# One hybrid gMLP and SSM layer on one core: gate and bias sums moved to VectorE, w_out's last weights and x fetched in another order, and a quarter of the last LayerNorm on two other engines

## Chip, cores and metric

The kernel runs on one core of a Trainium2 chip. The metric is the device time of one execution in microseconds, as the median of several runs.

## What is computed

One trunk layer of a diffusion backbone, all in fp32 on 1024 tokens of width 2048, with a context of 256 tokens in front. What matters here is the modulation by `c`, the bias of the spatial gating, and the end:

```python
mod_x = silu(c) @ w_ada + b_ada                      # c: (1, 2048), w_ada: (2048, 6144)
shift_x, scale_x, gate_x = split(mod_x, 3)
proj_x = modulate(layer_norm(x), shift_x, scale_x) @ w_in          # (1024, 5120)
...
# group A: gMLP, per head h of 8 and chunk of 128 positions
v = layer_norm(gelu(v)) * ln_g + ln_b
mixed = einsum("hpq,bnqhd->bnphd", w_s, v) + b_s
ya = gelu(u) * mixed * silu(za)
# group B: bidirectional S5 SSM over context and latents, D skip, GELU, GLU
yb = s5(ub, ub_ctx) * silu(zb)
out = concat([ya, yb]) @ w_out                       # (1024, 2048) @ (2048, 2048)
return layer_norm(ALPHA * x + gate_x * out) * ln_g + ln_b
```

The kernel takes `ln_b` of the gating through the spatial matrix ahead of time: what it adds to `mixed` for a head is `b_s` plus the row sums of `w_s` times `ln_b`. Those row sums are the "bias sums" here. The "gate row" is the third part of `mod_x`, 2048 numbers, needed only at the end.

## The kernel before

Every large matmul runs in three passes on split operands: a weight chunk of 128 x 1024 (512 KB) is loaded by SP's DMA queue into one of two raw buffers `wraw` (L565), ScalarE (ACT) copies it to a rounded `whi`, and VectorE (DVE) subtracts to get the rest, `wlo`. There are two buffers of each. `Weights` (L554) does this in the order of one list, `chunks`: `load_to(i)` issues loads up to chunk i, `split_to(i)` the splits. A load needs the raw buffer that the split two chunks earlier gave back. Per chunk TensorE (PE) then does 24 matmuls of 128x512.

The order of the program is: a prologue (modulation by `c`, LayerNorm of x), blocks of the input projection (`v`, `zb`, the context block `cx`, `ub`, then `v`, `u`, `za` and `zb` in turn), the spatial gating, the GLU, and the out stage. Side work is written as Python generators in a list `tasks`; `pump` takes the next step of these after every few main matmuls, so each engine's instruction order is fixed when the program is built. A generator says how far it wants to be behind: `until(t)` yields until a modelled clock of PE (`ck.pe`) or VectorE (`ck.dve`) has come to t, `wait(n)` yields n times. All compute instructions go through one metering helper, so that their line in the profile is L519.

`bias_task` (L1045) runs in the context stage: it loads the transposed spatial matrix `ws`, sums it over partitions with two fp32 matmuls against a matrix of ones (tile `io` in the rows, into a `sy` bank), and adds the result to `b_sp` by eight VectorE instructions. `gate_task` (L1062) runs in the last `zb` blocks: GpSimd's queue loads `w_gate` in 32 pieces `gw` of 128x1024 (input rows on partitions), VectorE accumulates them, each times one column of scalars `sc`, into `acc`, and four fp32 ones-matmuls into `ps` sum over the partitions. The row goes to a scratch in DRAM, from which the out stage loads it.

The out stage is two halves h of four token tiles of 128, and in each half four blocks n = 0, 2, 4, 6 of 512 output columns (`out_block`, L1426, 8 chunks each, 192 matmuls). The first half's results are taken through the residual and LayerNorm by `ln_task` during the second half, with ScalarE for the normalizing and, for the last step of it, GpSimd's addition of `lnb` over 128x1024, and written out by L1503 in pieces of 1 MB. At chunk 0 of each block `flush` issues the residuals that are left of the block before, and `gate(n)` then loads the gate columns `gt` (L1417) on SP's queue; there is one `gt` buffer, so the load waits for the last residual of the block before, and what stands behind it on the queue waits too. `z1_task` loads x for the second half: eight pieces of 128x1024 on SP's queue, one per two steps of `pump`, in block n=0 of the second half.

The last block (h=1, n=6) is done token tile by token tile. For that its eight chunks of `w_out` have to be split and kept ahead of time, in one tile `w6`. Their loads are interleaved with those of block n=4 one to one, so n=4 loads and splits 16 chunks. For each tile t = 4 to 7 comes the residual of its last quarter, the LayerNorm factors (`ln_finish`), and `finish`: for each stretch of columns one VectorE instruction `z<-z,lnw,lng` and one `z<-z,lnw,lnb` (scalar-tensor-tensor with a column of scalars `lnw`), then the output DMA. The last tile takes 1024, 512 and 512 columns.

Of the kernel before, what the change touches and what calls it, by code (L numbers as in the profile page):

```python
# [24 lines left out]
def dap(t, offset, ap):  # L25
    return bass.AP(tensor=t.tensor, offset=t.offset + offset, ap=[list(a) for a in ap])
# [559 lines left out]
def build(tc, a, out, scratch):  # L586
    nc = Metered(tc.nc)
    ck = nc.clock
    V, S, T, P, SP = nc.vector, nc.scalar, nc.tensor, nc.gpsimd, nc.sync
# [13 lines left out]
    def bank(tag, bufs):  # L603
        return (sb[1] if tag == "sb" else pp).tile([128, 512], FT, name=tag, tag=tag, bufs=bufs)
# [16 lines left out]
    def add(key, src):  # L621
        first[key] = len(chunks)
        chunks.append(src)
# [8 lines left out]
    for h in range(2):  # L632
        for n in range(0, 8, 2):
            if (h, n) != (1, 6):
                for c in range(8):
                    add(("out", h, n, c), a["w_out"][n // 2, c])
                    if (h, n) == (1, 4):
                        add(("out", 1, 6, c), a["w_out"][3, c])
    W = Weights(nc, wpool, chunks)
    last, w6 = [first["out", 1, 6, c] for c in range(8)], []  # L640

# [26 lines left out]
    tasks = []  # L668
# [366 lines left out]
    o = block(("v", 3))  # L1035
# [6 lines left out]
    cl_es.close()  # L1042
    us_es = ExitStack()
    us_p = us_es.enter_context(tc.tile_pool(name="us", bufs=2))
    def bias_task():  # L1045

        ws = st_p.tile([128, 8, 128], FT, name="ws", tag="sta")
        P.dma_start(ws, dap(a["w_sp"], 0, [[128, 128], [16384, 8], [1, 128]]))
        bs = st_p.tile([128, 8, 128], FT, name="bs", tag="stb")
        P.dma_start(bs, dap(a["b_sp"], 0, [[0, 128], [128, 8], [1, 128]]))  # L1050
        yield from until(ck.pe + 20000)
        for h0 in (0, 4):
            rs = bank("sy", 1)
            T.matmul(rs, ones, ws[:, h0:h0 + 4].rearrange("p h d -> p (h d)"), start=True, stop=True)
            yield from wait(2)
            for h in range(h0, h0 + 4):
                V.scalar_tensor_tensor(bs[:, h], rs[:, 128 * (h - h0):128 * (h - h0) + 128], vecs[:, 1, h:h + 1],
                                       bs[:, h], op0=OP.mult, op1=OP.add)
            yield from until(ck.pe + 4000)
        S.dma_start(dap(scratch["bp"], 0, [[128, 128], [16384, 8], [1, 128]]), bs)  # L1060

    def gate_task(p):  # L1062

        for c in range(2):
            cols = slice(1024 * c, 1024 * c + 1024)
            acc = p.tile([128, 1024], FT, name="acc")
            w = {}

            def load(i):
                w[i] = p.tile([128, 1024], FT, name="gw", bufs=4)  # L1070
                P.dma_start(w[i], a["w_gate"][i * 128:i * 128 + 128, cols])
            for i in range(3):
                load(i)
            yield from until(ck.pe + 3500)
            for i in range(16):
                if i < 13:
                    load(i + 3)
                if i:
                    V.scalar_tensor_tensor(acc, w[i], sc[:, 0, i:i + 1], acc, op0=OP.mult, op1=OP.add)
                else:  # L1080
                    V.tensor_scalar(acc, w[0], sc[:, 0, 0:1], None, op0=OP.mult)
                yield from wait(1 + i % 2)
            br = p.tile([128, 1024], FT, name="gw", bufs=4)
            SP.dma_start(br[0:1], a["b_gate"][None, cols])
            yield from until(ck.dve + 4000)
            for h in halves:
                ps = bank("ps", 1)
                T.matmul(ps, ones, acc[:, h], start=True, stop=True)
                yield from until(ck.pe + 1000)
                V.tensor_add(br[0:1, h], ps[0:1], br[0:1, h])  # L1090
            SP.dma_start(scratch["gate"][None, cols], br[0:1])


    tasks.append(bias_task())
    for m in range(8):
        e = bank("sb", 2)
        for c in range(2):
# [14 lines left out]
    us_es.close()  # L1112
    cx_es.close()
    ub_m = []


    def ub_there(u):
# [308 lines left out]
    def out_block(h, n, z):  # L1426

        o = [bank(*x) for x in ((("mm", 4),) * 4 if n % 4 else
                                (("sb", 2), ("sb", 2), ("ps", 1), ("sy", 1)))]
        for c in range(8):  # L1430
            if (h, n) == (1, 4):
                i = first["out", h, n, c]
                hl = W.get(i)
                W.load_to(i + 1)
                if c == 4:
                    drain(lt)
                    w6.append(z0_p.tile([128, 8, 1024], FR, name="w6", tag="z0", bufs=1))
                W.split_to(i + 1)
                W.load_to(i + 3)
                W.split_to(min(i + 2, last[7]))  # L1440
            else:
                hl = wget(("out", h, n, c))
            if c == 0:
                flush()
                gt = gate(n)
            w = [[x[:, 512 * kk:512 * kk + 512] for x in hl] for kk in range(2)]
            for i in range(4):
                for j in range(2):
                    kk, t = (i // 2, 2 * (i % 2) + j) if c < 7 else (j, i)
# [64 lines left out]
    for t in range(4, 8):  # L1514
        o = bank("mm", 4)
        for c in range(8):
            for kk in range(2):
                out_mm(o, (8 + 2 * c + kk) % 16, [x[:, kk * 512:kk * 512 + 512] for x in wts[c]], t,
                       c == 0 and kk == 0, c == 7 and kk == 1)
        residual(6, t, z1[t - 4, 1][:, 512:1024], o, gt)  # L1520
        ln_finish(t, t + 1)
        for i, x, y in ((0, 0, 1024), (1, 0, 1024)) if t < 7 else ((0, 0, 1024), (1, 0, 512), (1, 512, 1024)):
            z, c = z1[t - 4, i][:, x:y], slice(1024 * i + x, 1024 * i + y)
            for _ in finish(t, z, c, False):
                pass
            SP.dma_start(out[t * 128:t * 128 + 128, c], z)
# [6 lines left out]
def host(i):  # L1533

    C = np.ascontiguousarray
    o = s5_host(i)
    o["x"], o["ctx"] = C(i["x"][0]), C(i["ctx"][0])
    o["cc"] = C(np.stack([i["c"][0].reshape(16, 128).T, i["c_ctx"].reshape(16, 128).T], axis=1))
    w = i["w_ada"][0]

    w2 = w[:, :4096].reshape(4, 4, 128, 2, 8, 256)
    o["w_mod"] = C(w2.transpose(4, 0, 2, 1, 3, 5).reshape(8, 4, 128, 4, 512))
    o["w_gate"] = C(w[:, 4096:])
    b = i["b_ada"][0]
    o["b_mod"] = C(b[:4096].reshape(2, 8, 2, 128).transpose(3, 1, 0, 2).reshape(128, 8, 4))
    o["b_gate"] = C(b[4096:])
# [6 lines left out]
    o["w_sp"] = C(i["w_spatial"][0].transpose(0, 2, 1))  # L1553
    o["b_sp"] = C(i["b_spatial"][0])
    o["ln_g"], o["ln_b"] = C(i["ln_g"][0]), C(i["ln_b"][0])
    return o


SCRATCH = dict(gate=(2048,), bp=(8, 128, 128), pf=(8, G, 2, 128), tab=(2, 128, G, F), z5=(G, 16, 2, 144), ub=(G, 16, 8, KL), ubc=(G, 16, 8, KC), y5=(1024, 1024),
               v=(8, 128, 8, 128), ya=(8, 128, 1024), sz=(8, 128, 1024))  # L1560


# [21 lines left out]
```

## Time and profile before

| | us |
|---|---|
| median of 3 runs | 1612.44 (1611.13 to 1613.03) |
| the profiled execution | 1615.11 |
| its span, first to last instruction | 1613.3 |
| PE busy | 1567.1 |
| DVE, ACT, POOL busy | 1077.7, 504.3, 185.5 |
| out stage, second half, blocks n = 0, 2, 4, 6 | 44.83, 44.72, 49.51, 43.51 |
| from the last matmul to the end | 12.8 |

PE is the engine with work nearly all the time; matmuls of 512 columns follow each other every 0.2266 us at the full granted clock. Rows of one timeline that carry a count (x2) stand for neighbours of the same form put together; the time of such a row runs to the modelled end of the last of them, which overlaps the start of the next row. A bracket at a row's end is the idle time before it and what ended it.

### The profile page before, as it was taken

The numbers are of one execution on the slowest core, as the hardware profiler recorded it, in microseconds if no ns is written. First come the engines' busy times: TensorE is split into PE (matmuls) and PEld (weight loads), VectorE is DVE, ScalarE is ACT, GpSimd is POOL, SyncE is SP. The second block draws the span as 40 slices with busy tenths as digits, with TensorE's granted clock in tenths as the row PEclk, the third lists the DMA queues.
The fourth block names the chain that finished last, engine by engine and source line by source line (L and its number), as shares of the span: only waits on it lengthen the run. The fifth ranks groups of instructions, "written<-read, shape, count | busy, mean of one in ns | idle before, by whom it ended". The sixth has DMA issues, their size and how long they took to land.

```text
span 1613.3 us, 22086 instructions
## 1 busy us (share of the span) xinstructions
PE 1567.1 (97%) x8340; PEld 1260.7 (78%) x8340; DVE 1077.7 (67%) x1968; ACT 504.3 (31%) x832; POOL 185.5 (11%) x288
## 2 busy tenths in 40 slices
PE   4999999999999999999999999999999999999996
PEld 2556878887888888888888888888888888877775
DVE  8542646973988889888898898156565633466557
ACT  2554652112222333233233323211633412133210
POOL 0000000000222222222222222111000000012000
PEclk9999999999999999999999999999999999999998
DMA  9895454424454444444434443377544543364422
GB/s 336 323 325 173 161 173 144 148 109 127 109 125 128 114 128 129 100 127 128 127 98 128 129 117 90 138 248 248 190 143 170 196 137 124 107 230 179 137 86 104
DMA packets 133316, 251.36 MB, mean 156 GB/s; under 512 B 53973, under 2 KB 73557, under 8 KB 131417
## 3 DMA queue, kind: packets, MB, share of 16 engines
q1 hardware_dynamic: 111016, 207.68, 39.6%
q0 software_dynamic: 16672, 32.83, 7.2%
q10 hardware_dynamic: 5520, 9.44, 1.7%
q8 instruction: 65, 1.06, 0.3%
q14 instruction: 43, 0.34, 0.1%
HBM read 213.60 MB, written 36.12 MB: 155 GB/s over the span
## 4 chain that ended last, share of the span: by engine, by line
PE 84%; DMA 6%; DVE 5%; ACT 2%; SPq 1%; issue 1%; ACTq 0%; DVEq 0%
PE mm L519 64%; PE sb L519 9%; PE sy L519 8%; PE ps L519 3%; DMA wraw<-in_w_out_dram 2%; DVE wlo L519 2%; DMA ada<-in_w_mod_dram 1%; ACT whi L519 1%; DVE z L519 1%; DVE stats L519 1%; DVE xn L519 1%; DMA xn<-in_x_dram 1%; DMA wraw<-in_w_in_dram 1%; DMA ubb<-in_b_c_dram 0%; DMA cl<-in_ctx_dram 0%
## 5 line engine op out<-in xcount | busy, mean ns | idle before, releaser
L519 PE MATMUL mm<-xT,whi 128*128 128x512 f32 x2496 | 687.2, 395 | 2.0 <-ACT whi L519 1.0
L519 PEld LDWEIGHTS mm<-xT,whi 128*128 128x128 f32 x2496 | 461.6, 188 | 108.8 <-issue 7.8
L519 PE MATMUL mm<-xT,wlo 128*128 128x512 f32 x1248 | 391.0, 390 | 0.1
L519 DVE TENSOR_TENSOR wlo<-wraw,whi 128x1024 fp32r<-128x1024 f32 (+1 forms) x164 | 201.1, 1228 | 275.8 <-ACT whi L519 275.0
L519 ACT ACTIVATE whi<-wraw 128x1024 fp32r<-128x1024 f32 (+1 forms) x164 | 170.1, 1039 | 403.9 <-PE mm L519 215.4
L519 PEld LDWEIGHTS mm<-xT,wlo 128*128 128x128 f32 x1248 | 234.3, 188 | 50.9 <-DVE wlo L519 1.4
L519 DVE TENSOR_TENSOR p<-sb,ue 128x640 f32<-128x640 f32 x64 | 49.8, 819 | 49.0 <-PE sb L519 48.9
L519 PE MATMUL mm<-whi,yb 128*128 128x512 f32 x256 | 80.0, 389 | 0.0
L519 PE MATMUL mm<-y,whi 128*128 128x512 f32 x256 | 68.4, 389 | 0.0
L519 POOL TENSOR_TENSOR zs<-zs,dsk 128x16 f32<-128x16 f32 x32 | 17.7, 552 | 424.3 <-ACT zs L519 424.3
L519 PE MATMUL mm<-whi,ya 128*128 128x512 f32 x192 | 59.6, 389 | 0.0
L519 PE MATMUL sy<-ada,cs 128*32 128x512 f32 x256 | 40.5, 645 | 19.3 <-DMA ada<-in_w_mod_dram 19.2
L519 POOL TENSOR_TENSOR z<-z,lnb 128x1024 f32<-128x1024 f32 x8 | 19.2, 2397 | 347.1 <-DMA z<-in_x_dram 312.3
L519 PEld LDWEIGHTS mm<-y,whi 128*128 128x128 f32 x256 | 48.0, 188 | 10.0
L519 PEld LDWEIGHTS mm<-whi,yb 128*128 128x128 f32 x256 | 48.1, 188 | 10.0
L519 DVE TENSOR_TENSOR xT<-xm,xT 128x512 fp32r<-128x512 f32 x32 | 22.1, 692 | 45.9 <-ACT xT L519 44.3
L519 PE MATMUL mm<-wlo,yb 128*128 128x512 f32 x128 | 49.9, 390 | 0.4 <-DVE wlo L519 0.4
L519 DVE TENSOR_TENSOR_SCAN p<-ur,p 128x640 f32<-128x640 f32 x32 | 47.7, 1490 | 3.0 <-DVE ut L519 0.5
L519 PE MATMUL sb<-whi,yb 128*128 128x512 f32 x128 | 45.4, 396 | 1.4 <-ACT whi L519 1.4
L519 PE MATMUL sb<-cT,whi 128*128 128x512 f32 x128 | 46.2, 401 | 0.1
L403 POOL DMA_DIRECT2D tmp_z<-zs x64 | 44.1, 691 | 11.4 <-POOL zs L519 9.1
L519 DVE TENSOR_TENSOR p<-p,ue 128x512 f32<-128x512 f32 x64 | 44.2, 690 | 1.7
(274 smaller groups left out, 2313.2 us busy)
## 6 DMA issues: line engine op xcount, KB each, us to landing
wraw<-in_w_in_dram SPq DMA_DIRECT2D x89, 512.0 KB
ada<-in_w_mod_dram SPq DMA_DIRECT2D x64, 512.0 KB
wraw<-in_w_out_dram SPq DMA_DIRECT2D x64, 512.0 KB
gw<-in_w_gate_dram POOLq DMA_DIRECT2D x32, 512.0 KB, 5.8
xn<-in_x_dram SPq DMA_DIRECT2D x16, 512.0 KB
upf<-tmp_pf SPq DMA_DIRECT2D x32, 256.0 KB
ubb<-in_b_c_dram SPq DMA_DIRECT2D x32, 256.0 KB
tmp_v<-vt ACTq DMA_DIRECT2D x8, 512.0 KB
```

The costliest lines, as they stand in the source:

```text
L403: nc.gpsimd.dma_start(dap(d["z5"], (z["g0"] + q) * 32 * 144, [[72, 2], [144, 32], [1, 72]]), zs[64 * q:64 * q + 64])
L519: r = f(*args, **kw)
```

## The change

It has five parts. (a) `bias_task` loads the spatial matrix untransposed (`w_spn`, position on partitions), VectorE reduces it along the free axis to eight columns, `rows` transposes these on PE, copies by ScalarE and writes to a scratch `rs`; a broadcasting load and eight VectorE instructions follow. The task joins the list behind the context stage. (b) `gate_task` loads `w_gate` transposed in 16 pieces of 128x2048 (outputs on partitions, three buffers) and `c` as a row on all partitions (`sr`, Silu by ScalarE); 32 `tensor_tensor_reduce` instructions on VectorE multiply and sum 1024 columns each into one number per partition; two small additions, a transpose by `rows`. (c) The eight chunks of the last block come behind the odd chunks of n=2 and of n=4, four in each. (d) The x loads come one per four steps, and the second four 44 steps later. (e) In the last token tile the columns 0 to 511 are normalized by ScalarE and multiplied and added by GpSimd, and written by ScalarE's queue; VectorE does the other three quarters in six passes of 512, after one instruction that makes a scalar for ScalarE.

```diff
@@ build @@
             if (h, n) != (1, 6):
                 for c in range(8):
                     add(("out", h, n, c), a["w_out"][n // 2, c])
-                    if (h, n) == (1, 4):
-                        add(("out", 1, 6, c), a["w_out"][3, c])
+                    if h and n and c % 2:
+                        add(("out", 1, 6, (n - 2) * 2 + c // 2), a["w_out"][3, (n - 2) * 2 + c // 2])
...
+    def rows(x, tag, to, rt):
+
+        n = x.shape[1]
+        pt = bank(tag, 1)
+        T.transpose(pt[:n, 0:128], x, ident)
+        yield from wait(2)
+        S.activation(rt, pt[:n, 0:128], AF.Copy)
+        yield from wait(2)
+        P.dma_start(to, rt)
+
     def bias_task():
...
-        yield from until(ck.pe + 20000)
-        for h0 in (0, 4):
-            rs = bank("sy", 1)
-            T.matmul(rs, ones, ws[:, h0:h0 + 4].rearrange("p h d -> p (h d)"), start=True, stop=True)
-            yield from wait(2)
-            for h in range(h0, h0 + 4):
-                V.scalar_tensor_tensor(bs[:, h], rs[:, 128 * (h - h0):128 * (h - h0) + 128], vecs[:, 1, h:h + 1],
-                                       bs[:, h], op0=OP.mult, op1=OP.add)
-            yield from until(ck.pe + 4000)
+        yield from until(ck.pe + 12000)
+        rs = cstat.rearrange("p a b -> p (a b)")[:, 0:8]
+        V.tensor_reduce(rs, ws, axis=AX.X, op=OP.add)
+        yield from until(ck.dve + 3000)
+        yield from rows(rs, "sy", scratch["rs"], ws[0:8, 0])
...
     def gate_task(p):
 
-        for c in range(2):
...
-            for i in range(16):
-                if i < 13:
-                    load(i + 3)
-                if i:
-                    V.scalar_tensor_tensor(acc, w[i], sc[:, 0, i:i + 1], acc, op0=OP.mult, op1=OP.add)
-                else:
-                    V.tensor_scalar(acc, w[0], sc[:, 0, 0:1], None, op0=OP.mult)
-                yield from wait(1 + i % 2)
...
-            for h in halves:
-                ps = bank("ps", 1)
-                T.matmul(ps, ones, acc[:, h], start=True, stop=True)
-                yield from until(ck.pe + 1000)
-                V.tensor_add(br[0:1, h], ps[0:1], br[0:1, h])
-            SP.dma_start(scratch["gate"][None, cols], br[0:1])
...
-    tasks.append(bias_task())
+        sr = p.tile([128, 2048], FT, name="sr")
+        P.dma_start(sr, dap(a["c_row"], 0, [[0, 128], [1, 2048]]))
...
+        def load(i):
+            w[i] = p.tile([128, 2048], FT, name="gw", bufs=3)
+            P.dma_start(w[i], a["w_gate"][i])
...
+        for i in range(16):
+            if i < 14:
+                load(i + 2)
+            for h in range(2):
+                c = slice(1024 * h, 1024 * h + 1024)
+                V.tensor_tensor_reduce(w[i][:, c], w[i][:, c], sr[:, c], scale=1.0, scalar=0.0, op0=OP.mult,
+                                       op1=OP.add, accum_out=acc[:, i, h:h + 1])
+                yield from wait(1 + h)
...
+        yield from until(ck.dve + 2000)
+        yield from rows(bg, "ps", scratch["gate"].rearrange("(a b) -> a b", b=128), sr[0:16, 0:128])
...
@@ out_block @@
-            if (h, n) == (1, 4):
+            if h and n and c % 2:
                 i = first["out", h, n, c]
                 hl = W.get(i)
-                W.load_to(i + 1)
-                if c == 4:
+                W.load_to(i + 2)
+                if (n, c) == (4, 1):
                     drain(lt)
                     w6.append(z0_p.tile([128, 8, 1024], FR, name="w6", tag="z0", bufs=1))
                 W.split_to(i + 1)
                 W.load_to(i + 3)
-                W.split_to(min(i + 2, last[7]))
+                W.split_to(i + 2 if i + 1 < last[7] else i + 1)
...
@@ z1_task @@
                 SP.dma_start(z1[t, i], a["x"][512 + t * 128:640 + t * 128, 1024 * i:1024 * i + 1024])
-                yield
-                yield
+                yield from wait(4)
+            yield from wait(44)
...
@@ the last token tile @@
-        for i, x, y in ((0, 0, 1024), (1, 0, 1024)) if t < 7 else ((0, 0, 1024), (1, 0, 512), (1, 512, 1024)):
+        if t == 7:
+
+            z, c = z1[3, 0][:, 0:512], slice(0, 512)
+            V.scalar_tensor_tensor(lnw[:, 7, 4:5], lnw[:, 7, 0:1], -1.0, lnw[:, 7, 2:3], op0=OP.mult, op1=OP.mult)
+            S.activation(z, z, AF.Identity, bias=lnw[:, 7, 4:5], scale=lnw[:, 7, 2:3])
+            P.tensor_mul(z, z, lng[:, c])
+            P.tensor_add(z, z, lnb[:, c])
+            S.dma_start(out[t * 128:t * 128 + 128, c], z)
+        for i, x, y in ((0, 0, 1024), (1, 0, 1024)) if t < 7 else ((0, 512, 1024), (1, 0, 512), (1, 512, 1024)):
```

What the instruction order makes of this at three places. On PE, in the `zb` block where the gate's first half is summed, `mm` are the main matmuls, `acc` the accumulated products and `io` the ones; before:

```order
L519 MATMUL mm<-xT,whi 128x512 x4
L519 MATMUL mm<-xT,wlo 128x512 x2
L519 MATMUL ps<-acc,io 128x512
L519 MATMUL mm<-xT,whi 128x512 x4
L519 MATMUL mm<-xT,wlo 128x512 x2
L519 MATMUL ps<-acc,io 128x512
```

and the one place on PE where the gate stands now, the transpose of `bg`:

```order
L519 MATMUL mm<-xT,whi 128x512 x4
L519 MATMUL mm<-xT,wlo 128x512 x2
L519 MATMUL ps<-io,bg 16x128
L519 MATMUL mm<-xT,whi 128x512 x4
L519 MATMUL mm<-xT,wlo 128x512 x2
```

Four insertions of 512 columns have become one of 128 rows. On SP's queue around the gate row's load `gt` of the second half's block n=2, the `wraw` rows before are chunks 1 and 2, then 3 behind `gt`, then 4 and 5:

```order
L565 DMA wraw_12055<-in_w_out_dram 128x1024
L565 DMA wraw_12098<-in_w_out_dram 128x1024
L1417 DMA gt_12112<-tmp_gate 128x512
L565 DMA wraw_12140<-in_w_out_dram 128x1024
L1503 DMA out_0_dram<-z0_10047 128x2048
L565 DMA wraw_12174<-in_w_out_dram 128x1024
L565 DMA wraw_12207<-in_w_out_dram 128x1024
```

and now they are chunk 1, the first chunk of the last block, then 2 and 3 behind `gt`, then the second chunk of the last block:

```order
L565 DMA wraw_12009<-in_w_out_dram 128x1024
L565 DMA wraw_12052<-in_w_out_dram 128x1024
L1428 DMA gt_12066<-tmp_gate 128x512
L565 DMA wraw_12094<-in_w_out_dram 128x1024
L565 DMA wraw_12100<-in_w_out_dram 128x1024
L1514 DMA out_0_dram<-z0_10009 128x2048
L565 DMA wraw_12134<-in_w_out_dram 128x1024
```

Chunk 2 has moved from ahead of `gt` to behind it. On VectorE the last instructions of the program, with the last tile's columns 0 to 1023 and 1024 to 2047 as two buffers, before:

```order
L519 SCALAR_TENSOR_TENSOR z_11873<-z_11873,lnw,lng 128x1024
L519 SCALAR_TENSOR_TENSOR z_11873<-z_11873,lnw,lnb 128x1024
L519 SCALAR_TENSOR_TENSOR z_11946<-z_11946,lnw,lng 128x512
L519 SCALAR_TENSOR_TENSOR z_11946<-z_11946,lnw,lnb 128x512
L519 SCALAR_TENSOR_TENSOR z_11946<-z_11946,lnw,lng 128x512
L519 SCALAR_TENSOR_TENSOR z_11946<-z_11946,lnw,lnb 128x512
```

and now:

```order
L519 SCALAR_TENSOR_TENSOR lnw<-lnw 128x1
L519 SCALAR_TENSOR_TENSOR z_11888<-z_11888,lnw,lng 128x512
L519 SCALAR_TENSOR_TENSOR z_11888<-z_11888,lnw,lnb 128x512
L519 SCALAR_TENSOR_TENSOR z_12441<-z_12441,lnw,lng 128x512
L519 SCALAR_TENSOR_TENSOR z_12441<-z_12441,lnw,lnb 128x512
L519 SCALAR_TENSOR_TENSOR z_12441<-z_12441,lnw,lng 128x512
L519 SCALAR_TENSOR_TENSOR z_12441<-z_12441,lnw,lnb 128x512
```

Of the tile's 2048 columns, each passed twice, VectorE has kept 1536; the two passes over the other 512 stand at the end of GpSimd's list:

```order
L519 TENSOR_TENSOR z_11888<-z_11888,lng 128x512
L519 TENSOR_TENSOR z_11888<-z_11888,lnb 128x512
```

## Rows read from the trace of the kernel before

**Rows 1.** The page: the span, and busy time of each engine with its instructions.

```profile
span 1613.3 us, 22086 instructions
PE 1567.1 (97%) x8340; PEld 1260.7 (78%) x8340; DVE 1077.7 (67%) x1968; ACT 504.3 (31%) x832; POOL 185.5 (11%) x288
```

**Rows 2.** The table of waits of PE: engine, tile, releaser, total us, times, longest.

```profile
PE sy L519 <- DMA ada<-in_w_mod_dram: 19.2, 3, 18.6
PE sb L519 <- DVE wlo L519: 4.2, 7, 0.8
```

**Rows 3.** Timeline of PE, context stage: start us, us, engine, line, operation, tiles.

```profile
235.06 0.28 PE L519 MATMUL sb<-cT,wlo 128*128 128x256 f32 x1
...
236.27 0.28 PE L519 MATMUL sb<-cT,wlo 128*128 128x256 f32 x1
```

**Rows 4.** Timeline of PE beside the gate's sums, in a zb block.

```profile
1084.42 0.62 PE L519 MATMUL mm<-xT,wlo 128*128 128x512 f32 x2
1084.88 1.02 PE L519 MATMUL ps<-acc,io 128*128 128x512 f32 x2
...
1086.67 0.63 PE L519 MATMUL mm<-xT,wlo 128*128 128x512 f32 x2
```

**Rows 5.** Timeline of PE: four transposes in the SSM stage.

```profile
529.77 0.60 PE L519 MATMUL ps<-io,vg 128*128 128x128 f32 x4
```

**Rows 6.** Groups by line, VectorE (DVE), tile acc: count, ns min/median/max, first and last start.

```profile
L519 DVE SCALAR_TENSOR_TENSOR acc<-gw,sc,acc x30: 1276/1285/1286, 1048.6 to 1124.6; 128x1024 f32<-128x1024 f32 x30
```

**Rows 7.** The page's costliest groups: the scan on VectorE (busy us, mean ns).

```profile
L519 DVE TENSOR_TENSOR_SCAN p<-ur,p 128x640 f32<-128x640 f32 x32 | 47.7, 1490 | 3.0 <-DVE ut L519 0.5
```

**Rows 8.** Stretch with gate loads: length, busy of five engines, granted clock, DMA share, GB/s.

```profile
1090.00:1120.00 30.00, 30.00 (x134) 24.82 (x133) 19.82 (x17) 4.71 (x6) 6.89 (x13) 1.00 0.88 299
```

**Rows 9.** Stretches of the out stage's second half: four blocks, then 5 us of one.

```profile
1417.91:1462.74 44.83, 43.98 (x192) 35.72 (x192) 27.90 (x36) 15.52 (x15) 11.98 (x5) 1.00 0.64 229
1462.74:1507.46 44.72, 44.13 (x193) 35.88 (x192) 24.33 (x32) 12.79 (x12) 7.20 (x3) 1.00 0.43 158
1507.46:1556.97 49.51, 46.52 (x194) 37.02 (x193) 26.67 (x32) 14.84 (x14) 0.00 (x0) 0.97 0.44 144
1556.97:1600.48 43.51, 43.51 (x192) 35.69 (x191) 30.15 (x56) 0.61 (x3) 0.00 (x0) 1.00 0.19 76
1520.00:1525.00 5.00, 4.24 (x11) 3.17 (x12) 2.37 (x2) 1.52 (x2) 0.00 (x0) 0.66 0.48 144
```

**Rows 10.** Timeline of PE in block n=4, second half.

```profile
1519.93 0.50 PE L519 MATMUL sb<-whi,yb 128*128 128x512 f32 x1 [1.43 <-ACT whi L519]
1521.19 0.80 PE L519 MATMUL sb<-wlo,yb 128*128 128x512 f32 x1 [0.76 <-DVE wlo L519]
```

**Rows 11.** Timeline of SP's queue in block n=2: the gate row's load.

```profile
1470.79 0.33 SPq L1417 DMA_DIRECT2D gt<-tmp_gate  x1
```

**Rows 12.** Chain of waits in n=2: start us, us, what; the load behind it.

```profile
1471.22 6.14 DMA wraw<-in_w_out_dram
```

**Rows 13.** Chain of waits in n=4: one chunk of weights.

```profile
1518.82 1.06 ACT whi L519
...
1519.91 1.24 DVE wlo L519
...
1521.16 3.27 DMA wraw<-in_w_out_dram
```

**Rows 14.** Timeline of VectorE at the end: the first and last of six passes.

```profile
1604.45 1.28 DVE L519 SCALAR_TENSOR_TENSOR z<-z,lnw,lng 128x1024 f32<-128x1024 f32 x1
...
1609.19 0.75 DVE L519 SCALAR_TENSOR_TENSOR z<-z,lnw,lnb 128x512 f32<-128x512 f32 x1
```

**Rows 15.** Groups by line, GpSimd (POOL), tile z.

```profile
L519 POOL TENSOR_TENSOR z<-z,lnb x8: 2391/2398/2406, 1430.6 to 1482.2; 128x1024 f32<-128x1024 f32 x8
```

**Rows 16.** Timeline of GpSimd and VectorE in block n=0 of the second half.

```profile
1458.02 2.40 POOL L519 TENSOR_TENSOR z<-z,lnb 128x1024 f32<-128x1024 f32 x1 [3.55 <-ACT z L519]
...
1458.92 2.58 DVE L519 TENSOR_TENSOR wlo<-wraw,whi 128x1024 fp32r<-128x1024 f32 x1 [2.17 <-ACT whi L519]
```

More of the change, by code (lines that the diff above doesn't have):

```diff
@@ L1044, in build @@
     us_p = us_es.enter_context(tc.tile_pool(name="us", bufs=2))
+    def rows(x, tag, to, rt):
[6 more added lines that the diff above has]
+        P.dma_start(to, rt)
     def bias_task():
         ws = st_p.tile([128, 8, 128], FT, name="ws", tag="sta")
-        P.dma_start(ws, dap(a["w_sp"], 0, [[128, 128], [16384, 8], [1, 128]]))
+        P.dma_start(ws, dap(a["w_spn"], 0, [[128, 128], [16384, 8], [1, 128]]))
@@ new lines, in bias_task @@
+        rs = cstat.rearrange("p a b -> p (a b)")[:, 0:8]
+        V.tensor_reduce(rs, ws, axis=AX.X, op=OP.add)
+        yield from until(ck.dve + 3000)
+        yield from rows(rs, "sy", scratch["rs"], ws[0:8, 0])
+        yield from until(ck.pe + 8000)
+        P.dma_start(ws, dap(scratch["rs"], 0, [[0, 128], [128, 8], [1, 128]]))
+        yield from until(ck.pe + 8000)
+        for h in range(8):
+            V.scalar_tensor_tensor(bs[:, h], ws[:, h], vecs[:, 1, h:h + 1], bs[:, h], op0=OP.mult, op1=OP.add)
+            yield
@@ L1060, in bias_task @@
         S.dma_start(dap(scratch["bp"], 0, [[128, 128], [16384, 8], [1, 128]]), bs)
     def gate_task(p):
-        for c in range(2):
[L1065 to L1074, printed above, removed]
-            for i in range(16):
-                if i < 13:
-                    load(i + 3)
-                if i:
-                    V.scalar_tensor_tensor(acc, w[i], sc[:, 0, i:i + 1], acc, op0=OP.mult, op1=OP.add)
-                else:
-                    V.tensor_scalar(acc, w[0], sc[:, 0, 0:1], None, op0=OP.mult)
-                yield from wait(1 + i % 2)
-            br = p.tile([128, 1024], FT, name="gw", bufs=4)
-            SP.dma_start(br[0:1], a["b_gate"][None, cols])
-            yield from until(ck.dve + 4000)
-            for h in halves:
-                ps = bank("ps", 1)
-                T.matmul(ps, ones, acc[:, h], start=True, stop=True)
-                yield from until(ck.pe + 1000)
-                V.tensor_add(br[0:1, h], ps[0:1], br[0:1, h])
-            SP.dma_start(scratch["gate"][None, cols], br[0:1])
@@ L1094, in build @@
-    tasks.append(bias_task())
+        sr = p.tile([128, 2048], FT, name="sr")
+        P.dma_start(sr, dap(a["c_row"], 0, [[0, 128], [1, 2048]]))
+        bg = p.tile([128, 16], FT, name="bg")
+        P.dma_start(bg, a["b_gate"])
+        acc = p.tile([128, 16, 2], FT, name="acc")
+        w = {}
+        def load(i):
+            w[i] = p.tile([128, 2048], FT, name="gw", bufs=3)
+            P.dma_start(w[i], a["w_gate"][i])
+        for i in range(2):
+            load(i)
+        yield from until(ck.pe + 3500)
@@ new lines, in gate_task @@
+        S.activation(sr, sr, AF.Silu)
+        yield
+        for i in range(16):
[6 more added lines that the diff above has]
+                yield from wait(1 + h)
+        V.tensor_add(bg, bg, acc[:, :, 0])
+        V.tensor_add(bg, bg, acc[:, :, 1])
@@ L1114, in build @@
     ub_m = []
+    tasks.append(bias_task())
     def ub_there(u):
@@ L1542, in host @@
     o["w_mod"] = C(w2.transpose(4, 0, 2, 1, 3, 5).reshape(8, 4, 128, 4, 512))
-    o["w_gate"] = C(w[:, 4096:])
+    o["w_gate"] = C(w[:, 4096:].T).reshape(16, 128, 2048)
+    o["c_row"] = C(i["c"][0])
     b = i["b_ada"][0]
     o["b_mod"] = C(b[:4096].reshape(2, 8, 2, 128).transpose(3, 1, 0, 2).reshape(128, 8, 4))
-    o["b_gate"] = C(b[4096:])
+    o["b_gate"] = C(b[4096:].reshape(16, 128).T)
     o["vecs"] = C(np.stack([i[n][0].reshape(8, 128).T for n in ("sgu_ln_g", "sgu_ln_b", "b_glu")], axis=1))
@@ L1553, in host @@
     o["w_sp"] = C(i["w_spatial"][0].transpose(0, 2, 1))
+    o["w_spn"] = C(i["w_spatial"][0])
     o["b_sp"] = C(i["b_spatial"][0])
@@ L1556, in host @@
     return o
-SCRATCH = dict(gate=(2048,), bp=(8, 128, 128), pf=(8, G, 2, 128), tab=(2, 128, G, F), z5=(G, 16, 2, 144), ub=(G, 16, 8, KL), ubc=(G, 16, 8, KC), y5=(1024, 1024),
+SCRATCH = dict(gate=(2048,), rs=(8, 128), bp=(8, 128, 128), pf=(8, G, 2, 128), tab=(2, 128, G, F), z5=(G, 16, 2, 144), ub=(G, 16, 8, KL), ubc=(G, 16, 8, KC), y5=(1024, 1024),
                v=(8, 128, 8, 128), ya=(8, 128, 1024), sz=(8, 128, 1024))
```

## The prediction

> **What bounds the kernel now.** I read the page first. TensorE (PE) is busy 1567.1 of 1613.3 us, so the end is set by the sum of its instructions plus the few places where it stands still [rows 1]. The table of what PE waits for says how few these are: 19.2 us at the start on the modulation weights, which the change does not touch, then 4.2 us on `wlo` (VectorE's half of the weight split) for the `sb` banks [rows 2]. From the first projection block to the out stage there is practically no wait. So in the middle of the program a PE instruction that goes away shortens the span by its full length and an instruction on another engine costs nothing as long as nobody waits for it. In the out stage the stretches by block show where time is lost: 192 matmuls take 43.51 us in the last block (0.2266 us each), and the three blocks before it in the second half, which I call n=0, 2 and 4, take 44.83, 44.72 and 49.51, that is 1.3, 1.2 and 6.0 us more [rows 9]. After the last matmul comes 12.8 us of VectorE and output transfer, which lie wholly on the path.
>
> The profiled execution has a span of 1613.3 us and a time of 1615.11, 2.67 above the median of 1612.44. I make the sum on the profile and take the difference off the median.
>
> **Bias sums.** Two fp32 matmuls with a matrix of ones go. Around the first of them PE goes from one 256-column matmul to the same one two steps later in 236.27-235.06 = 1.21 us [rows 3]; without the insertion a 512 and a 256 column matmul take 1.5 x 0.2266 = 0.34. One costs 0.87; two, 1.7 us. In their place VectorE reduces 128x1024 (a pass of about 1.3 us, from the accumulating rows of the same size [rows 6]), PE does a transpose of 8 columns, and a round trip through DRAM goes over GpSimd's queue. The task moves from the context stage to the `ub` stage behind it. Its consumers come hundreds of microseconds later, and VectorE's pass is covered by weights that were split ahead; cost 0, at worst one late `wlo` (0.8 us is the longest such wait [rows 2]).
>
> **Gate row.** Four ones-matmuls go. From one pair of `wlo` matmuls to the next is 1086.67-1084.42 = 2.25 us with one of them in between [rows 4], where six plain ones take 1.36: 0.89 each, 3.55 us together. Two transposes come in, one here and one for the bias: four of 128x128 last 0.60 us [rows 5], so 0.15 each, +0.3. VectorE's 30 accumulating passes of 1.285 us [rows 6] become 32 multiply-and-reduce passes over 128x1024. No row of before has that instruction. The nearest is the accumulating one, two inputs of the same size, 1.285; the far bound is the scan, which takes 1490 ns for 640 elements [rows 7], and would make 2.4 us of 1024. I take 1.3 to 1.45 (with an accumulator read behind it), because it too has one result per element and nothing in it depends on the element before. The bytes are the same 16 MB in loads of 1 MB; DMA is at 0.88 of its time here already [rows 8], so the loads can end neither much earlier nor later. By the order the new transpose stands some 2.6 us of PE work behind the point where I have the last pass done, so it is the place where a late gate would hold PE.
>
> [...]
>
> **Last quarter of w_out and the x loads.** This is the part with two signs. A chunk of weights goes load, ScalarE copy (1.06 us), VectorE subtract (1.24) [rows 13], and the next load needs the raw buffer back, of which there are two. Block n=4 handles 16 chunks in 43.5 us before, one each 2.72 us; the load alone takes 3.3 to 6.1 us [rows 12, 13]. [...] Now n=2 and n=4 take 12 chunks each, one per 3.6 us, which the chain meets (5.5 to 7.3 us for two). I give n=4 1.6 us of stalls instead of 6.0: -4.4.
>
> In n=2 it turns around. SP's queue holds the load of the gate row `gt`, which waits until VectorE is done with the old one: it goes at 1470.79 [rows 11], 8 us into the block. Before, the weights queued behind it are those of chunk 3, first needed at 1462.74 + 3 x 5.44 = 1479.1. Now an extra chunk stands in the place ahead of it, and what waits behind `gt` is chunk 2, needed at 1473.6. Issued at 1471.2, with a load of 3.3 us, the copy and the subtract, its `whi` is there about 1475.8 and its `wlo` at 1476.9. PE stops there for about 3.2 us. The stops of 2.2 us in n=4 cost 1.7 more by the clock, and I take the same here, with 0.4 for the following chunk, and drop the old 1.2: +4.1. In n=0 the eight x loads (512 KB each) are no longer ahead of the weights, and its idle time of 44.83-43.98 = 0.85 goes: -0.8. Net: -0.8 + 4.1 - 4.4 = -1.1. The bounds: if chunk 2 comes in time, -6; if n=4 keeps its stalls and n=2 gets its own, +5.
>
> **The tail.** Before: from 1604.45 two passes of 1024 and four of 512 columns end at 1609.94 [rows 14], and 3.3 us of output follow. Now VectorE begins with a one-column instruction (0.19), does six passes of 512 at a pitch of 0.743, and ends at about 1609.1, 0.8 earlier, if it is left alone. But ScalarE hands its quarter to GpSimd, which multiplies and adds on 128x512. GpSimd's row of 1024 takes 2398 ns [rows 15], so two of 512 take 2.4 to 2.6. Where such an instruction meets one of VectorE on two SBUF inputs, one stands still: the subtract that takes 1.24 shows 2.58 us, from 1458.92 to 1461.50, one pass behind GpSimd's end at 1460.42 [rows 16]. So the eight passes run one after the other: 1604.64 + 4.46 + 2.58 = 1611.7 instead of 1609.94, +1.7.
>
> [...]
>
> **Sum:** -1.7 - 3.55 + 0.3 - 1.1 + 1.7 = -4.4 us. On the profile 1615.1 becomes 1610.7; on the median 1612.44 - 4.4 = 1608.0.
>
> **Rivals.**
> 1. The out stage and the tail come out as meant. For it: n=2 has 1.2 us of loss to begin with and only half of the extras; the old wait behind `gt` has 8 us of slack. Against it: the order puts chunk 2 behind `gt`. -1.7 - 3.55 + 0.3 = -5, then -6 in the out stage and -0.8 to +1.7 in the tail: 1600.5 to 1603.
> 2. The queue in n=2 costs more than n=4 gives back: chunk 2's load takes the 6.1 us of [rows 12] instead of 3.3, so +3 more, and a longer run at the lower clock. With +5 in the out stage: -5 + 5 + 1.7 = +1.7, 1614. The one instruction that decides is `gt`'s load: if it goes later than about 1471, each microsecond is one of PE.
> 3. The slower side: multiply-and-reduce at 2.4 us. A chunk of the gate then needs 4.8 us of VectorE beside its weight splits, VectorE falls about 3.5 us behind for each of the last six chunks, and the slack of some 2.5 per chunk from weights split ahead gives way; `wlo` and the transpose would hold PE for 10 to 15 us: 1618 to 1623. It decides from about 1.7 us per pass.
> 4. The gate's loads end late: at 0.88 of the DMA's time [rows 8], a load of 1 MB in three buffers leaves less room than four of 512 KB; PE then waits 0 to 5 us at the transpose: 1608 to 1613.
>
> **How the numbers follow.** The sum 0.48, rival 1 0.22, rival 2 0.16, rival 3 0.08, rival 4 0.06. About 0.2% (3.2 us) is what a measurement of this kernel tells from no change: faster is below 1609.2, slower above 1615.7. The sum's own spread is about 3 us, so it gives faster two times in three: 0.32 + 0.22 + 0.02 = 0.56, slower 0.08 from rival 3, 0.05 from rival 2 and 0.01 beyond: 0.14, same 0.30. The range leaves out rival 3 and the lower end of rival 1: 1602 to 1615.5.
>
> **What would show it.** No ones-matmul between main matmuls and PE busy 5 us lower until the out stage: the first two terms. A multiply-and-reduce row of 1.3 to 1.45 us and no wait of PE on `bg`: the third and fourth rivals out. A wait of PE on `whi` about 11 us into n=2 with a granted clock below 1 behind it, and n=4 near 45 us: the out stage as summed; n=2 near 44.5 would be rival 1, above 50 rival 2. [...] I am wrong if the span moves by more than the range with these rows unchanged.

## The result: 0.5% slower

The changed kernel takes 1618.96 us in the median of 8 runs (1616.24 to 1622.03), the kernel before 1611.85 in 8 runs (1607.00 to 1613.76). The ratio is 1.0051, with a 95% interval of 1.0040 to 1.0063: about 8 us slower, where 4.4 us faster was forecast and 1615.5 was the upper end of the range. The profiled execution took 1619.64 us with a span of 1617.8, 4.5 more than the span before. (The profiled execution before was 3.3 us above its own median of these runs, that of after 0.7, which is most of the difference between the two comparisons.) Part of it lies in the start of the program. The first matmul of the context stage, up to which the diff changes nothing, before and now:

```profile
211.60 0.39 PE L519 MATMUL sb<-cT,whi 128*128 128x512 f32 x1
209.49 0.39 PE L519 MATMUL sb<-cT,whi 128*128 128x512 f32 x1
```

Over the profiles of all runs below, whatever the kernel, it stands between 207.3 and 211.6 us, so these 2.1 us are not the change's.

The page of the changed kernel, its span and the busy times, against [rows 1]:

```profile
span 1617.8 us, 22043 instructions
PE 1564.7 (97%) x8330; PEld 1262.7 (78%) x8330; DVE 1077.0 (67%) x2000; ACT 509.9 (32%) x838; POOL 182.8 (11%) x279
```

What PE waits for, against [rows 2] (releaser, total us, times, longest):

```profile
PE sy L519 <- DMA ada<-in_w_mod_dram: 19.7, 2, 18.9
PE mm L519 <- ACT whi L519: 6.4, 3, 3.2
PE sb L519 <- ACT whi L519: 3.5, 1, 3.5
...
PE sb L519 <- DVE wlo L519: 2.5, 5, 0.8
```

PE is busy 2.4 us less, although some of its matmuls ran slowly. What is new are three long waits for `whi`, the first half of a weight split: 3.2 us near 392, 2.6 in block n=2 and 3.5 in n=4. The four blocks of the out stage's second half and 7 us behind the last of these waits, against [rows 9]:

```profile
1414.89:1458.90 44.01, 43.81 (x193) 35.91 (x192) 29.04 (x38) 15.53 (x15) 11.98 (x5) 1.00 0.53 190
1458.90:1509.07 50.17, 47.14 (x194) 37.77 (x193) 29.20 (x33) 15.84 (x15) 7.17 (x3) 0.93 0.54 185
1509.07:1559.95 50.88, 46.94 (x193) 37.90 (x192) 23.00 (x31) 11.44 (x11) 0.00 (x0) 0.93 0.41 134
1559.95:1603.63 43.68, 43.68 (x193) 35.85 (x191) 29.79 (x55) 0.61 (x3) 0.00 (x0) 1.00 0.19 75
1523.00:1530.00 7.00, 5.95 (x13) 4.38 (x14) 2.45 (x2) 2.37 (x3) 0.00 (x0) 0.53 0.68 238
```

Cut at the first matmul of each block in the same way, the blocks before are 44.99, 44.72 and 49.35 us, so n=0 has won 0.98, n=2 has lost 5.45 and n=4 1.53. The granted clock of 0.93 over 50 us is that of about 7 us in each of the two blocks: microsecond by microsecond it reads 0.50 from 1473 to 1479 and from 1524 to 1530, 0.63 to 0.96 in the ones just before and behind, and 1.00 outside. From 1527.14 to 1530.13 seven matmuls of 512 columns start 0.427 us apart, where it is 0.2266 at 1.00. By the granted clock I estimate (1 - 0.93) x 50 = 3.5 us in each block, beside the wait itself. The tail, from the last matmul to the end, is 1617.8 - 1603.63 = 14.2 us against 12.8. All that lies ahead of the second half of the out stage ends 2.9 us earlier than before. Together: -2.9 - 1.0 + 5.4 + 1.5 + 1.4 = +4.4 of the 4.5 us. But 2.1 of the 2.9 are those of the start; from there to the second half the changed kernel has won 0.8 us, where the forecast had 5.0.

**The two waits in the out stage.** The timeline of PE in n=2, then the chain of waits that ends there (start us, us, what):

```profile
1472.51 0.79 PE L519 MATMUL mm<-whi,yb 128*128 128x512 f32 x1 [2.57 <-ACT whi L519]
1473.77 0.79 PE L519 MATMUL mm<-wlo,yb 128*128 128x512 f32 x1 [0.47 <-DVE wlo L519]
```

```profile
1465.72 0.61 DVE sy L519
...
1466.35 0.33 SPq L1428
...
1466.78 4.52 DMA wraw<-in_w_out_dram
...
1471.40 1.06 ACT whi L519
```

VectorE's last residual of the old block frees `gt`, SP's queue goes on (L1428), and only then chunk 2 of the weights is loaded. That is the wait the prediction described. The same thing stands in n=4. PE, then SP's queue:

```profile
1523.58 0.80 PE L519 MATMUL sb<-whi,yb 128*128 128x512 f32 x1 [3.48 <-ACT whi L519]
1524.84 0.80 PE L519 MATMUL sb<-wlo,yb 128*128 128x512 f32 x1 [0.46 <-DVE wlo L519]
```

```profile
1515.08 0.33 SPq L1428 DMA_DIRECT2D gt<-tmp_gate  x1
1515.45 0.42 SPq L1489 DMA_DIRECT2D z<-in_x_dram  x1
1515.98 2.06 SPq L565 DMA_DIRECT2D wraw<-in_w_out_dram  x2
```

Here an x load goes between `gt` and chunk 2, and the chain shows 6.39 us for the load that starts at 1515.98, where it was 4.52 in n=2 and 3.27 in [rows 13].

**The wait at 392.** PE's wait and SP's queue in the changed kernel, and under them the same places before:

```profile
391.99 1.19 PE L519 MATMUL mm<-xT,whi 128*128 128x512 f32 x4 [3.19 <-ACT whi L519]
```

```profile
387.41 6.14 SPq L565 DMA_DIRECT2D wraw<-in_w_in_dram  x3
```

```profile
393.08 1.20 PE L519 MATMUL mm<-xT,whi 128*128 128x512 f32 x4 [0.34 <-ACT whi L519]
```

```profile
388.33 6.31 SPq L565 DMA_DIRECT2D wraw<-in_w_in_dram  x3
```

The weight load stands behind 23 loads of the SSM's first unit (five, then 18 of `uu`; the expectations below count 17 with twelve of `uu`), which come at the end of another chain: VectorE's tables, their transposes on PE, two ScalarE copies, their stores, then these loads one by one. That chain ended 0.9 us earlier than before. PE had come 3.9 us earlier (2.1 from the start of the program, 1.7 from the two ones-matmuls), and waited the difference. Before, it waited 0.34 us at this place: two chains met there with next to no slack.

That PE came earlier would not by itself make it wait, for the chain starts from transposes in PE's own order (`sb`). What has changed is their place in it. The chain of waits from the end of the context stage to these transposes, before, then now:

```profile
261.23 102.03 PE mm L519 x450
363.26 0.45 PE sb L519 x4
```

```profile
257.16 17.72 PE mm L519 x78
...
274.99 87.09 PE mm L519 x384
362.08 0.45 PE sb L519 x4
```

Now 462 main matmuls stand ahead of them instead of 450, and 12 take 2.7 us. The SSM's table generator goes by VectorE's modelled clock: it yields while that is more than 2.5 us ahead of PE's (`room`), and ahead of the transposes until PE's is 4 us past it (`until`). The bias task has brought 3.6 us of VectorE work into this stage: a reduction of 1.21 and eight multiply-and-adds of 2.35 together. Every run with the new bias sums has 462 matmuls there and every run without them 450; that they come by these two clocks is read from the program, and no run tests it by itself.

**The gate and the tail.** The group of the multiply-and-reduce (ns min/median/max, first and last start), where [rows 6] stood:

```profile
L519 DVE CUSTOM_DVE_ANT_0 gw<-gw,sr x32: 1218/1221/1227, 1049.1 to 1114.9; 128x1024 f32<-128x1024 f32 x32
```

1.22 us each, with an accumulator read of 0.08, and no wait of PE on `bg` or on VectorE in that stage. The last tile, VectorE and GpSimd:

```profile
1608.58 0.75 DVE L519 SCALAR_TENSOR_TENSOR z<-z,lnw,lnb 128x512 f32<-128x512 f32 x1
1608.80 1.64 POOL L519 TENSOR_TENSOR z<-z,lng 128x512 f32<-128x512 f32 x1 [124.31 <-ACT z L519]
1609.24 1.75 DVE L519 SCALAR_TENSOR_TENSOR z<-z,lnw,lng 128x512 f32<-128x512 f32 x1
1610.53 1.59 POOL L519 TENSOR_TENSOR z<-z,lnb 128x512 f32<-128x512 f32 x1
1611.03 1.63 DVE L519 SCALAR_TENSOR_TENSOR z<-z,lnw,lnb 128x512 f32<-128x512 f32 x1
...
1613.36 0.75 DVE L519 SCALAR_TENSOR_TENSOR z<-z,lnw,lnb 128x512 f32<-128x512 f32 x1
```

Two passes of VectorE read 1.75 and 1.63 instead of 0.75, and GpSimd's 1.64 and 1.59: they end in turn, at 1610.44 (GpSimd), 1610.99, 1612.12 (GpSimd) and 1612.66, as if whichever comes second were held until the other is done. [rows 16] had this for VectorE's subtract, at 2.58 us; here it is the two-input form with a column of scalars.

### The profile page after: what moved, and what is told of

It reads as the page before. It is cut to its first block, busy times and chain, and to the rows that moved or that the text cites. A ratio compares the mean times of both kernels' runs of the same rounds, so it can differ in the third digit from the quotient of the medians.

```text
span 1617.8 us, 22043 instructions
## 1 busy us (share of the span) xinstructions
PE 1564.7 (97%) x8330; PEld 1262.7 (78%) x8330; DVE 1077.0 (67%) x2000; ACT 509.9 (32%) x838; POOL 182.8 (11%) x279
## 3 DMA queue, kind: packets, MB, share of 16 engines
q8 instruction: 65, 1.06, 0.3%
## 4 chain that ended last, share of the span: by engine, by line
PE 84%; DVE 6%; DMA 4%; ACT 3%; SPq 1%; issue 1%; ACTq 0%; DVEq 0%
PE mm L519 62%; PE sb L519 10%; PE sy L519 8%; PE ps L519 4%; DMA wraw<-in_w_out_dram 2%; DVE wlo L519 2%; DVE z L519 1%; DVE stats L519 1%; ACT whi L519 1%; DVE xn L519 1%; ACT xm L519 1%; DMA xn<-in_x_dram 1%; DMA ada<-in_w_mod_dram 1%; DVE lnw L519 0%; DMA wraw<-in_w_in_dram 0%
## 5 line engine op out<-in xcount | busy, mean ns | idle before, releaser
L519 POOL TENSOR_TENSOR z<-z,lnb 128x1024 f32<-128x1024 f32 (+1 forms) x9 | 20.7, 2305 | 342.7 <-DMA z<-in_x_dram 305.0
```

The lines of the kernel that those rows point to most:

```text
L519: r = f(*args, **kw)
```

## The experiments

Ratios are against runs of the kernel before on the same chip. 1610 us times the ratio's distance from 1 gives the us.

### One part at a time

The first four each make one part of the change in the kernel before; their edits are the hunks of the diff shown ahead of the prediction. The bias sums:

```diff
-    tasks.append(bias_task())
...
+        V.tensor_reduce(rs, ws, axis=AX.X, op=OP.add)
...
     ub_m = []
+    tasks.append(bias_task())
```

> The kernel before with the bias sums alone changed (their task moved behind the context stage). My theory: the end does not move by the 1.7 us that the two ones-matmuls give back, because near 390 us a weight load stands on SP's queue behind the SSM's twelve uu loads, and the kernel before already waits 0.34 us there (393.08); PE that comes 1.6 us earlier waits about 1.9 us at that place, so 0 us in all, and up to 2 us slower if the granted clock falls behind the longer wait. Rival (the forecast's sum): 1.6 us faster, no longer wait at 390.

1.0028 (1.0018 to 1.0038): 4.5 us slower, more than either expected. PE's timeline and the 5 us behind the wait:

```profile
394.00 1.56 PE L519 MATMUL mm<-xT,whi 128*128 128x512 f32 x4 [2.85 <-ACT whi L519]
```

```profile
394.00:399.00 5.00, 5.00 (x15) 3.73 (x16) 4.90 (x10) 3.46 (x5) 0.53 (x1) 0.66 0.56 186
```

The wait has grown by 2.5 us and the granted clock is 0.66 over the 5 us behind it, by my estimate (1 - 0.66) x 5 = 1.7 us. Less the saved 1.6 this is 2.6 of the 4.5 us, a little below the interval's lower end of 2.9. Part of the rest comes from the one profile of before: from the first matmul of the context stage to the first of the out stage's second half this run takes 1208.6 us and the kernel before 1206.2, but the runs of the order of the last weights and of the last tile below, which run the same instructions as the kernel before up to there, take 1205.1 and 1205.0 and have no wait at this place. Against these the part costs 3.5 us. The wait is not, as my theory had it, PE that comes earlier to a chain that stands still: it is the transposes that stand 12 matmuls later.

The gate row:

```diff
-                T.matmul(ps, ones, acc[:, h], start=True, stop=True)
...
+                V.tensor_tensor_reduce(w[i][:, c], w[i][:, c], sr[:, c], scale=1.0, scalar=0.0, op0=OP.mult,
+                                       op1=OP.add, accum_out=acc[:, i, h:h + 1])
```

> The kernel before with the gate row alone changed. My theory and the forecast agree: PE loses four ones-matmuls of 0.89 us and gains a transpose of 0.15, 3.4 us faster, multiply-and-reduce rows of 1.3 to 1.5 us and no wait of PE on bg or on wlo in that stage. Rival: DMA or VectorE time of the gate is paid elsewhere in the zb blocks, 0 us.

0.9984 (0.9975 to 0.9993): 2.6 us faster, and the interval (1.1 to 4.0) holds the 3.4. The term stands.

The order of the last weights and of x:

```diff
-                    if (h, n) == (1, 4):
-                        add(("out", 1, 6, c), a["w_out"][3, c])
+                    if h and n and c % 2:
+                        add(("out", 1, 6, (n - 2) * 2 + c // 2), a["w_out"][3, (n - 2) * 2 + c // 2])
...
+            yield from wait(44)
```

> The kernel before with the order of the last weights and of x alone changed. My theory: chunk 2 of n=2 and chunk 2 of n=4 wait behind gt's load, PE stands 2 to 4 us at each with the granted clock lower behind both; n=0 near 44.0, n=2 near 50, n=4 near 51 us, together 6 us slower than before. Rival (the forecast): n=2 up by 4, n=4 down by 4.4, 1.1 us faster in all.

1.0044 (1.0030 to 1.0057): 7.1 us slower. Blocks n=0, 2 and 4 take 44.07, 49.58 and 50.28 us, with waits of 2.54 and 3.81 us for `whi` at chunk 2 of the latter two. My theory held; the forecast fell. (The slow matmuls, 0.427 us apart, last about 3.4 us in each of the two blocks here, from 1473.1 and from 1524.2, where it was 7 us in the changed kernel's profile.)

The last tile:

```diff
+            S.activation(z, z, AF.Identity, bias=lnw[:, 7, 4:5], scale=lnw[:, 7, 2:3])
+            P.tensor_mul(z, z, lng[:, c])
+            P.tensor_add(z, z, lnb[:, c])
```

> The kernel before with the last token tile alone changed. My theory: VectorE and GpSimd exclude each other, so the time from the last matmul to the end goes from 12.8 to 14.1 us, 1.3 us slower. Rival: the tail is 0.8 us faster, as six passes of 512 columns without hindrance would be, and what the changed kernel's tail lost came from what ran ahead of it.

1.0011 (1.0002 to 1.0019): 1.8 us slower (0.3 to 3.1), with a tail of 13.8 us. The four ratios add up to 1.0067, beside 1.0051 for all together, and within their intervals this is the same.

### The two queues mended

```diff
-        gt = z0_p.tile([128, 512], FT, name="gt", bufs=1)
+        gt = z0_p.tile([128, 512], FT, name="gt", bufs=2)
```

> The changed kernel with two buffers for the gate columns gt instead of one, so that their load need not wait for the last residual of the block before. My theory: SP's queue goes on at once, chunk 2 comes in time, the waits of PE about 11 us into n=2 and n=4 and the lower clock behind them go; n=2 near 44.5 and n=4 near 46 us, 9 to 11 us faster than the changed kernel. Rival: it is the bandwidth (x loads, 1 MB outputs and weights at once) that makes chunk 2 late; then the waits stay and it is within 2 us of the changed kernel.

0.9984 (0.9974 to 0.9994), against 1.0051 without the second buffer: 10.8 us, give or take some 2.5. The three blocks, and SP's queue at the start of n=2:

```profile
1412.42:1456.47 44.05, 43.87 (x193) 35.91 (x192) 29.03 (x38) 15.53 (x15) 11.98 (x5) 1.00 0.53 188
1456.47:1502.49 46.02, 44.70 (x194) 35.73 (x192) 27.67 (x31) 15.97 (x15) 7.21 (x3) 1.00 0.57 199
1502.49:1546.01 43.52, 43.52 (x194) 36.04 (x192) 23.46 (x32) 11.57 (x11) 0.00 (x0) 1.00 0.47 165
```

```profile
1455.02 0.42 SPq L1428 DMA_DIRECT2D gt<-tmp_gate  x1
1461.18 5.68 SPq L565 DMA_DIRECT2D wraw<-in_w_out_dram  x2
```

`gt` is loaded ahead of the block, chunk 2 goes 4.7 us into it instead of 7.9, and n=4 is down to its bare matmuls. So it was the wait for the buffer; the bandwidth alone does not make chunk 2 late. n=2 stays 2.5 us above its bare matmuls, with a granted clock of 1.00.

```diff
         s5.setup(sp, psum)
+        nl = W.nl
+        while W.nl == nl:
+            yield
         s5.load(0)
```

> The changed kernel with one thing moved: the first SSM unit's loads (17 on SP's queue) are issued behind the next weight load instead of ahead of it. My theory: the wait of 3.2 us at 392 and the lower clock behind it go, and the gain of the bias sums comes through; 4 to 5 us faster than the changed kernel. Rival: VectorE's table work paces that stage whatever the queue does, the SSM's first unit is only later, and another wait of like size comes instead; 0 us.

1.0015 (1.0007 to 1.0024): 5.8 us faster than the changed kernel. There is no wait of PE between 375 and 400 us and the matmuls keep their pitch there, six in 1.36 us. The 462 matmuls ahead of the transposes are the same, so it took both to make the wait: the SSM's loads that start later, and a weight load that stands behind them on the queue.

The same loop with the bias sums alone:

> The bias sums alone changed, with the weight load ahead of the SSM's first loads. My theory: the wait of 2.8 us at 390 and the lower clock behind it go, so it is 1 to 2 us faster than the kernel before, where the bias sums alone were 4.5 us slower. Rival: the wait only moves to the next chunk of weights; 2 to 4 us slower than before.

0.9994 (0.9984 to 1.0004). The 4.5 us are gone and the estimate is 1 us faster; the 1.6 us of the two ones-matmuls lie in the interval, and so does nothing. The profiles say 1.6: from the first matmul of the context stage to the first of the out stage's second half this run takes 1203.4 us, and the kernel before with both mends, below, 1205.0.

```diff
-        if t == 7:
-
-            z, c = z1[3, 0][:, 0:512], slice(0, 512)
...
-        for i, x, y in ((0, 0, 1024), (1, 0, 1024)) if t < 7 else ((0, 512, 1024), (1, 0, 512), (1, 512, 1024)):
+        for i, x, y in ((0, 0, 1024), (1, 0, 1024)) if t < 7 else ((0, 0, 1024), (1, 0, 512), (1, 512, 1024)):
```

This with both mends in the changed kernel:

> The changed kernel with two gt buffers, with the weight load ahead of the SSM's, and with the old last tile. My theory: the parts add, 10 + 4.5 + 1.5 us faster than the changed kernel, so 7 to 9 us faster than the kernel before. Rival (the forecast's second: the losses move to the next late thing on the same queues): no faster than the kernel before.

0.9945 (0.9932 to 0.9957), 1601.73 us beside 1610.57: 8.9 us faster than the kernel before. Both mends in the kernel before, without the change:

> The kernel before with the two mends alone (two gt buffers, weight load ahead of the SSM's first loads), none of the change. My theory: its block n=4 is late by loads that wait for raw buffers, not for gt, so it stays near 49 us and the two mends give 0 to 2 us; the rest of the gain of the mended kernel is the change's own. Rival: the mends are the whole gain, 7 to 9 us, and the change gives nothing beside them.

0.9983 (0.9974 to 0.9992): 2.7 us, a little more than I had given it; n=4 still takes 47.52 us there. So of the 8.9 us some 6 are the change's own, without its last tile: about 5 from the ones-matmuls (1199.9 us instead of 1205.0 between the same two matmuls as above), and in the out stage n=4 falls from 47.52 to 43.52 while n=2 rises from 43.63 to 46.33, 1.3 us in all on one profile each, too little for the run times to show alone. Block n=0 takes 44.03 us there with the x loads where they were and 44.02 in the mended kernel, so beside the second buffer moving them gives nothing.

### The tail's two engines

```diff
-            P.tensor_mul(z, z, lng[:, c])
-            P.tensor_add(z, z, lnb[:, c])
```

> The changed kernel without GpSimd's multiplication and addition in the last tile, so that a quarter of the last 128 rows is normalized only, not scaled by ln_g and ln_b. [...] Rival (the passes are slowed by ScalarE or by the output transfers): two passes still show 1.6 to 1.8 us.

From the last matmul to the end 12.2 us in its one execution, beside 14.2, and no pass over 0.75; ScalarE's quarter is still there. So it is GpSimd's two instructions that slow the passes. The whole change with both mends:

> The whole change, the last tile too, with the two mends. My theory: 1.2 us slower than the mended kernel with the old tail, 6 to 8 us faster than before; from the last matmul to the end 14.2 us. Rival: with the rest gone the tail's split costs nothing, as fast as the mended kernel.

0.9949 (0.9936 to 0.9961), tail 14.3 us, beside 0.9945 and 13.3 with the old last tile: the two times cannot be told apart. And VectorE's passes with one input in PSUM:

```diff
+            for i, (k, q, b) in enumerate((("sb", lng, 2), ("sb", lng, 2), ("ps", lng, 1), ("sy", lnb, 1), ("mm", lnb, 4), ("mm", lnb, 4))):
+                g[i] = bank(k, b)
+                S.activation(g[i], q[:, 512 * (i % 3) + 512:512 * (i % 3) + 1024], AF.Copy)
...
+                V.scalar_tensor_tensor(z, z, lnw[:, 7, 0:1], g[i], op0=OP.subtract, op1=OP.mult)
+                V.scalar_tensor_tensor(z, z, lnw[:, 7, 2:3], g[3 + i], op0=OP.mult, op1=OP.add)
```

> The whole change with the two mends, and VectorE's six last passes read ln_g and ln_b from PSUM, where ScalarE copies them while PE works on the last tile. My theory: with one input in PSUM VectorE and GpSimd no longer exclude each other; every pass takes 0.75 us while GpSimd works, from the last matmul to the end 12.2 to 12.6 us, 1.7 us faster than the whole change with the mends alone. Rival: the two exclude each other whatever the operands; passes of 1.6 to 1.8 us and 14.2 us.

The tail is 12.4 us. The timeline of both engines in it:

```profile
1593.64 0.75 DVE L519 SCALAR_TENSOR_TENSOR z<-z,lnw,sy 128x512 f32<-128x512 f32 x1
1593.87 1.27 POOL L519 TENSOR_TENSOR z<-z,lng 128x512 f32<-128x512 f32 x1 [116.69 <-ACT z L519]
1594.30 0.74 DVE L519 SCALAR_TENSOR_TENSOR z<-z,lnw,sb 128x512 f32<-128x512 f32 x1
1595.08 0.75 DVE L519 SCALAR_TENSOR_TENSOR z<-z,lnw,mm 128x512 f32<-128x512 f32 x1
1595.21 1.27 POOL L519 TENSOR_TENSOR z<-z,lnb 128x512 f32<-128x512 f32 x1
```

The same instructions side by side, at 0.75 and 1.27, where the changed kernel had 1.75 and 1.63 on VectorE and 1.64 and 1.59 on GpSimd: what has changed for these passes is VectorE's second input, from PSUM instead of SBUF. In time, 0.9945 (0.9932 to 0.9957) cannot be told from 0.9949; the 1.9 us are shown by the profile alone.

## Why the prediction was wrong

**The bias sums: the step that failed first.** The prediction said that in the middle of the program a PE instruction that goes away shortens the span by its full length "and an instruction on another engine costs nothing as long as nobody waits for it". It read "practically no wait" as slack, and priced what replaces the two matmuls at "cost 0". But PE's own wait of 0.34 us at 393, too small for the table's first lines, marked where the SSM's loads and the weights meet on SP's queue, and 3.6 us of new VectorE work in that stage went with a start of those loads 12 matmuls (2.7 us) later in PE's order. Instead of 1.7 us faster the part alone was 4.5 slower: a wait of 2.85 us and the granted clock of 0.66 over the 5 us behind it. With the weight load ahead of those loads it was no longer slower.

**The gate row: right.** -3.4 by the sum, -2.6 measured. The pass is 1.22 us, so the third rival falls; PE did not wait for the gate's loads either, so the fourth falls.

**The out stage: the mechanism was seen and stopped half-way.** For n=2 I had the wait behind `gt` and its size (3.0 us measured, 3.2 forecast), and n=0's gain (1.0 against 0.8). The sum took over from n=4 stops of 2.2 us and 1.7 more by the clock; these are read from [rows 9, 10], waits of 1.43 and 0.76 and 11 matmuls busy for 4.24 us, where 11 x 0.2266 are 2.5. That n=2 would pay the same 1.7 no row showed: the clock of 0.50 cost some 3.5 in the profile of the changed kernel, and the slow matmuls about 1.6 in that of this part alone, (1 - 0.2266/0.427) x 3.4. The term that failed is n=4's -4.4, measured +1.5; that 1.6 of the 6.0 us would be left was my estimate. I let it keep 1.6 us of stalls because the chain of loads had more time there, and did not put chunk 2 of n=4 through the same working as that of n=2. `gt` goes at 1515.08, 6 us into the block, an x load and a load of 6.39 us follow, and 1.6 us became 3.9, with the clock of 0.50 behind it. The time that the chain was said to have does not come out of the rows either: load, copy and subtract are 3.27 to 6.14, 1.06 and 1.24 us [rows 12, 13], so two chunks through two buffers take 5.6 to 8.4 us, not 5.5 to 7.3, and they had 7.3. And 3.3 us for a load was the quicker of the two rows; the two that counted took 4.52 and 6.39, and the one behind `gt` in n=4 of the kernel before had shown as much:

```profile
1514.21 4.51 DMA wraw<-in_w_out_dram
```

The second rival was this with the right sign, priced at +5 in the out stage; it was +6.0 in the profile, +7.1 in the runs. (The +5 is partly luck: n=4 with its old stalls and n=2 with its new ones are -0.8 + 4.1 = +3.3 by the prediction's own terms.)

**The tail: right in mechanism and nearly in size.** +1.7 by the sum, +1.4 on the profile, +1.8 in the runs of the part alone (about +1 on its profile).

So the sum -1.7 - 3.55 + 0.3 - 1.1 + 1.7 has two terms that were wrong, the first and the fourth, and both have a load on SP's in-order queue that stands behind another which comes late. The range ended too low mainly by the first: the second rival with all of its +5 came to 1614, and the bias term, which the prediction doubted by no more than one late `wlo` of 0.8 us, was off by 6.2.

## What to carry to other kernels

Before an instruction that goes from the busiest engine is counted as gain, find the next place at which that engine meets another chain, and its slack there; the mark here was a wait of 0.34 us. Where the instruction order is made by a model of the engines' clocks, work that moves to a spare engine also moves what is ordered by that engine's clock: count the place of the next chain's first instruction before and after. On a DMA queue that goes in order, as SP's did here (the load behind `gt` went 0.43 us after it), write down, for every load behind one that waits, when it is first needed, in each block that has the pattern and not only in the first. A second buffer of 128x512 for the tile that made the queue wait was worth 10.8 us here, more than the 5.0 that all the moved matmuls were to give.

## What was not expected of the hardware

Multiply-and-reduce on two fp32 inputs took 1.221 us for 1024 columns, less than the scalar-tensor-tensor pass of 1.285 that it replaced (the accumulator read behind it takes 0.083). A wait of 2.57 and 0.47 us was followed by about 7 us at a granted clock of 0.50 in n=2, one of 2.54 and 0.75 in the run with the out stage's order alone by 3.4 us of matmuls 0.427 apart, while the 0.37 and 0.76 us that the second buffer left there kept a granted clock of 1.00. And a VectorE pass with one input in PSUM took 0.75 us beside GpSimd's 1.27, where the same pass on SBUF took 1.75 and 1.63 beside GpSimd's 1.64 and 1.59.
